# Latent keys normed and rotated right behind their projection, and the memory keys' transposes moved behind the third head pair's values, in a two-layer mixer and FFN kernel

## The chip, the cores and the metric

One core of a Trainium2 chip runs the whole program. The metric is the time of one execution on the device in microseconds (us). Three runs of the kernel before took 1013.88, 1010.58 and 1015.88 us, median 1013.88; one more execution was taken with the hardware profiler, and all rows below come from it.

## The reference

256 tokens of width 1024, float32, pass two layers. The first is an FFN, a mixer of window attention and mLSTM, and a second FFN. The second layer, where the change lies, mixes gated linear attention (GLA, 4 heads) with latent attention (MLA, 8 heads), then attends to a memory of 256 tokens, and ends with a convolved FFN. What the change touches is this:

```python
q = to_heads(rms_norm_2(c_q, mla_q_a_norm[l]) @ mla_w_uq[l], MLA_HEADS)
kv = to_heads(rms_norm_2(c_kv, mla_kv_a_norm[l]) @ mla_w_ukv[l], MLA_HEADS)
k_nope, v = kv[..., :MLA_NOPE], kv[..., MLA_NOPE:]
k_rot = jnp.broadcast_to(k_pe[:, None], (b, MLA_HEADS, s, MLA_ROPE))
k = jnp.concatenate([k_nope, k_rot], axis=-1)
q = rms_norm_2(q, mla_q_norm[l])
k = rms_norm_2(k, mla_k_norm[l])
q = jnp.concatenate([q[..., :MLA_NOPE], rope(q[..., MLA_NOPE:], positions)], axis=-1)
k = jnp.concatenate([k[..., :MLA_NOPE], rope(k[..., MLA_NOPE:], positions)], axis=-1)
o_mla = from_heads(causal_block_attention(q, k, v))
...
xk = rms_norm_2(xkv[:, :, 0], xa_k_norm[l])
```

## The kernel before, in words

Every large product is made of weights that stream from memory as float32, are split into a high half on ScalarE (line 368) and a low half on VectorE (line 369), and are multiplied three times on TensorE: lines 388 to 393 where features lie on the partitions, lines 397 to 399 (`mm3n`) where tokens do. Vectors of reciprocal roots are worked out by eleven small steps on GpSimd (`rsqrt`, lines 450 to 465).

The change lies in `mix2_heads` (lines 1056 to 1370). The latents are projected first (line 1066). Then come the latent keys without their rotated part, `pk` (line 1129), whose squares are summed per head into half 1 of `ssq` (line 1133), and the latent queries `q` in two halves of four heads (loop at line 1134), whose squares are summed into half 0 (line 1141). Both halves get a norm term (line 1142) and share one reciprocal root, `rqk` (line 1143). Behind it `kn`, the normed keys of all heads, is written: the plain part from `pk` (line 1150), the rotated part from `kp` (line 1152). The queries are rotated in one go (line 1154); their root `rq` enters later, with the scores.

The heads are worked on in four pairs by three helpers. `turned` transposes a pair's queries and keys (line 1190) and copies them to `qT` on VectorE (line 1193) and to `kT` on ScalarE (line 1195). `scores` multiplies them (lines 1205 and 1206), adds mask and scale and finds maxima on VectorE (lines 1210 and 1211), and takes exponentials on ScalarE (lines 1214 and 1215). `values` transposes the weights (line 1227), copies them to `pT` on ScalarE (line 1229), multiplies them with the values (line 1234) and splits the result. Between these steps stand the dense products `og`, `uv` and `gv`, the memory's keys `xk` (`xa_keys`, line 1398), the GLA products with the chunk states `st` (lines 1311 to 1322), and the GLA outputs `po` (lines 1342 to 1346). `xa_turn` (line 1415) transposes the memory's keys (line 1421) and copies them to `xkT` (line 1422), which the cross attention after this stage reads.

PSUM is dealt from two pools. `pa()` gives one bank out of four (tag "at"); the products of the latent keys and queries, the transposes and the scores use it. `bank()` gives one half of a two-bank tile out of two such tiles (tag "mm"), in the order in which the code calls it; the dense products, `xa_turn`, the states and `po` use it.

The order on each engine is not that of the text. The program is built in a context that simulates the time of every instruction (line 1582); whichever instruction is ready, has its buffer and comes first in the text is put next on its engine. `queued` (line 319) adds a rule to that: what is traced inside it on an engine comes behind the engine's instruction that was traced last before it. Each engine then works through its own queue in order. The weights' DMAs are issued by SP (line 354).

Of the kernel before, what the change touches and what calls it, by code (L numbers as in the profile page):

```python
# [14 lines left out]
AF = mybir.ActivationFunctionType  # L15
ALU = mybir.AluOpType
AX = mybir.AxisListType
PSUM = bass.MemoryType.PSUM

P = 128  # L20
# [3 lines left out]
TB = T // P  # L24
# [163 lines left out]
class Builder:  # L188
# [867 lines left out]
    def mix2_heads(self, mp, ot, xs, ms):  # L1056
        nc = self.nc
        V = nc.vector
# [4 lines left out]
        H = 8  # L1063


        ps = self.lin_n("lat", 432, xs)
# [9 lines left out]
        cs_ = []  # L1076
# [20 lines left out]
        ad = mt([P, 2, TB], "ad")  # L1097
# [28 lines left out]
        q = mt([P, TB, H, 96], "q")  # L1126
        ssq = mt([P, 2, TB, H], "ssq")
        rqk = mt([P, 2, TB, H], "rqk")
        pk = self.lin_n("uk", 512, cs_[:1], 1, pool=self.pa)
        for b in range(TB):  # L1130
            s2 = self.tmp([P, 512], "z")
            nc.scalar.activation(s2, pk[b], AF.Square)
            V.tensor_reduce(ssq[:, 1, b, :], s2.rearrange("p (h d) -> p h d", h=H), op=ALU.add, axis=AX.X)
        for c in range(2):
            ps = self.lin_n(f"uq{c}", 384, cs_[1:], 2, pool=self.pa)
            for b in range(TB):
                qb = q[:, b, 4 * c:4 * c + 4, :].rearrange("p h d -> p (h d)")
                nc.scalar.activation(qb, ps[b][:, :384], AF.Copy)
                s2 = self.tmp([P, 512], "z")
                nc.scalar.activation(s2[:, :384], ps[b][:, :384], AF.Square)  # L1140
                V.tensor_reduce(ssq[:, 0, b, 4 * c:4 * c + 4], s2[:, :384].rearrange("p (h d) -> p h d", h=4), op=ALU.add, axis=AX.X)
        V.tensor_tensor(ssq, ssq, ad[:, :, :, None].to_broadcast([P, 2, TB, H]), ALU.add)
        self.rsqrt(rqk, ssq, [P, 2, TB, H])
        rq, rk = rqk[:, 0], rqk[:, 1]
        kp = mt([P, TB, 32], "kp")
        self.rope(kp, cz[:, :, 384:416], "gk", lambda t: t, [P, TB, 32])
        rkp = mt([P, TB, H], "rkp")
        V.tensor_tensor(rkp, rk, fp[:, :, None].to_broadcast([P, TB, H]), ALU.mult)
        for b in range(TB):
# [1 line left out]
                            rk[:, b, :, None].to_broadcast([P, H, 64]), ALU.mult)  # L1151
            V.tensor_tensor(kn[:, b, :, 64:96], kp[:, b, None, :].to_broadcast([P, H, 32]),
                            rkp[:, b, :, None].to_broadcast([P, H, 32]), ALU.mult)
        self.rope(q[:, :, :, 64:96], q[:, :, :, 64:96], "gq", lambda t: t[:, :, None, :].to_broadcast([P, TB, H, 32]), [P, TB, H, 32])


        w2 = mt([16, T], "w2")
# [41 lines left out]
        def scores(qT, hp):  # L1199
            qT, kT = qT  # L1200
            out = []
            for i in range(2):
                h = 2 * hp + i
                ps = self.pa()
                nc.tensor.matmul(ps[:, 0:P], qT[:, i * T:i * T + P], kT[:, i * T:i * T + P], start=True, stop=True)
                nc.tensor.matmul(ps[:, P:3 * P], qT[:, i * T + P:i * T + T], kT[:, i * T:i * T + T], start=True, stop=True)
                S = mt([P, 3 * P], "S2", bufs=3)
                m = self.tmp([P, TB], "m2")
                wm = self.wmask.rearrange("p a k -> p (a k)")
                V.tensor_tensor_reduce(S[:, 0:P], ps[:, 0:P], wm[:, P:2 * P], rq[:, 0, h:h + 1], -3.0e38, ALU.add, ALU.max, m[:, 0:1])  # L1210
                V.tensor_tensor_reduce(S[:, P:3 * P], ps[:, P:3 * P], wm[:, 2 * P:4 * P], rq[:, 1, h:h + 1], -3.0e38, ALU.add, ALU.max, m[:, 1:2])
                V.tensor_scalar(m, m, -1.0, None, ALU.mult)
                l = self.tmp([P, TB], "l2")
                nc.scalar.activation(S[:, 0:P], S[:, 0:P], AF.Exp, bias=m[:, 0:1], accum_out=l[:, 0:1])
                nc.scalar.activation(S[:, P:3 * P], S[:, P:3 * P], AF.Exp, bias=m[:, 1:2], accum_out=l[:, 1:2])
                V.reciprocal(l, l)
                V.tensor_scalar(S[:, 0:P], S[:, 0:P], l[:, 0:1], None, ALU.mult)
                V.tensor_scalar(S[:, P:3 * P], S[:, P:3 * P], l[:, 1:2], None, ALU.mult)
                out.append(S)
            return out  # L1220

        def values(hp, Ss):
            pTs = []
            for i in range(2):
                pt = self.pa()
                for k in range(3):
                    nc.tensor.transpose(pt[:, k * P:k * P + P], Ss[i][:, k * P:k * P + P], self.ident)
                pT = mt([P, 3 * P], "pT2", bufs=2)
                nc.scalar.activation(pT, pt[:, :3 * P], AF.Copy)
                pTs.append(pT)  # L1230
            po = self.pa()
            for q0, kb, first, last in ((0, 0, True, True), (P, 0, True, False), (P, 1, False, True)):
                for i in range(2):
                    nc.tensor.matmul(po[64 * i:64 * i + 64, q0:q0 + P], vv[:, kb, 2 * hp + i, :],
                                     pTs[i][:, kb * P + q0:kb * P + q0 + P], start=first, stop=last)
            ms[4 + hp] = ot([P, 2, T], f"mla{hp}", dt=F32R)
            self.split(ms[4 + hp], po[:, :T])
# [5 lines left out]
        ps = self.lin_n("og", 512, xs)  # L1243
        for b in range(TB):
            nc.scalar.activation(og[:, b, :], ps[b], AF.Copy, scale=rN[:, b:b + 1])
        ps = self.lin_n("uv", 512, cs_[:1], 1)
# [15 lines left out]
        ps = self.lin_n("gv", 512, xs)  # L1262
# [5 lines left out]
        xkT = ot([P, 4, T], "xkT")  # L1268
        kk = self.xa_keys(ts, g2)
# [27 lines left out]
        S2 = scores(q2, 2)  # L1297
        q3 = turned(3)
        values(1, S1)
        self.xa_turn(kk, xkT)  # L1300


        st = [None]
        for c in range(3):
            b, c2 = c // 2, c % 2
# [19 lines left out]

        S3 = scores(q3, 3)
        values(2, S2)


        for b in range(TB):  # L1330
# [6 lines left out]
        for b in range(TB):  # L1337
            pt = po[b]
            for j in range(2):
# [4 lines left out]
                for r in range(2):  # L1344
                    h = 2 * j + r
# [11 lines left out]
        for hp in range(2):  # L1357
            pt = self.pa()
            for i in range(2):
                for b in range(TB):  # L1360
                    h = 2 * hp + i
# [225 lines left out]
```

## Time and profile before

| what | value |
|---|---|
| median of three runs | 1013.88 us |
| lowest and highest run | 1010.58 and 1015.88 us |
| profiled execution | 1010.23 us |
| its span, from first to last instruction | 1008.5 us |
| TensorE, VectorE, ScalarE, GpSimd busy in it | 98%, 73%, 59%, 6% |
| mean granted TensorE clock | 0.996 of full speed |
| share of TensorE in the chain of work that ended last | 94% |

How to read it: PE is TensorE's matmuls, PEld its weight loads, which overlap them, DVE is VectorE, ACT ScalarE, POOL GpSimd. Times in rows are us from the start of the span. [...] A row such as `714.89 0.77 PE L1205 MATMUL at<-kT,qT ... x2 [3.24 <-DVE qT L1193]` says that from 714.89 on two matmuls of line 1205, from kT and qT into an "at" bank, ran for 0.77 us together, and that TensorE had been idle for 3.24 us before, until VectorE's line 1193 was done. Matmuls are pipelined and overlap, so the busy times of single ones add up to more than the time they take together.

### The profile page before, as it was taken

How to read it: one execution, taken by the hardware profiler on the slowest of the kernel's cores; microseconds unless marked ns; L12 is line 12 of the kernel's file. 1: busy time of each engine (PE TensorE's matmuls, PEld its weight loads, DVE VectorE, ACT ScalarE, POOL GpSimd, SP SyncE). 2: the span in 40 equal slices, each digit the busy share in tenths (PEclk: the TensorE clock that was granted, in tenths of full speed). 3: DMA queues.
4: the chain of work that ended last, by engine and by line, in shares of the span. 5: the costliest groups of instructions: out<-in, count | busy, mean ns of one | idle time of the engine just before them, and what ended most of it. 6: DMA issues, size and time to landing. Idle time of an engine off the chain costs nothing.

```text
span 1008.5 us, 15805 instructions
## 1 busy us (share of the span) xinstructions
PE 984.3 (98%) x5870; PEld 856.2 (85%) x5870; DVE 737.8 (73%) x1288; ACT 596.4 (59%) x1038; POOL 59.4 (6%) x195
## 2 busy tenths in 40 slices
PE   7999999999999999999999999999899999999998
PEld 6888888988677788888888888998789888888887
DVE  7777766668986577776777865778858668888662
ACT  7655544568854556545655644659846457666541
POOL 2100000010000010001000200012001301000000
PEclk9999999999999999999999999999899999999999
DMA  8655555555345345545555655556306336555550
GB/s 298 251 188 190 182 187 183 196 168 179 125 154 182 105 141 194 189 169 169 200 184 191 211 180 174 170 195 206 103 1 219 116 105 217 191 191 177 182 172 21
DMA packets 51405, 172.80 MB, mean 171 GB/s; under 512 B 6256, under 2 KB 7552, under 8 KB 51328
## 3 DMA queue, kind: packets, MB, share of 16 engines
q1 hardware_dynamic: 49536, 169.89, 49.5%
q10 hardware_dynamic: 1728, 1.88, 0.8%
q8 instruction: 46, 0.75, 0.3%
q14 instruction: 31, 0.25, 0.1%
q0 software_dynamic: 64, 0.02, 0.0%
HBM read 170.72 MB, written 1.05 MB: 170 GB/s over the span
## 4 chain that ended last, share of the span: by engine, by line
PE 94%; DVE 3%; ACT 1%; issue 1%; POOL 0%; DMA 0%; DVEq 0%; ACTq 0%
PE mm L392 41%; PE mm L393 21%; PE mm L397 3%; PE mm L398 3%; PE mm L399 3%; PE mm L389 3%; PE mm L388 3%; PE mm L390 3%; PE at L392 2%; PE at L748 1%; PE at L708 1%; DVE wl L369 1%; PE at L393 1%; ACT wh L368 1%; PE at L740 1%
## 5 line engine op out<-in xcount | busy, mean ns | idle before, releaser
L369 DVE TENSOR_TENSOR wl<-wr,wh 128x1024 fp32r<-128x1024 f32 (+5 forms) x376 | 389.9, 1051 | 193.6 <-ACT wh L368 189.0
L368 ACT ACTIVATE wh<-wr 128x1024 fp32r<-128x1024 f32 (+5 forms) x376 | 339.1, 918 | 312.6 <-PE mm L392 149.0
L392 PE MATMUL mm<-xs,wh 128*128 128x512 f32 x1264 | 444.4, 395 | 2.4 <-DVE s L546 1.5
L393 PE MATMUL mm<-xs,wl 128*128 128x256 f32 x1264 | 354.8, 281 | 0.0
L392 PEld LDWEIGHTS mm<-xs,wh 128*128 128x128 f32 x1264 | 237.0, 187 | 58.2 <-issue 2.4
L393 PEld LDWEIGHTS mm<-xs,wl 128*128 128x128 f32 x1264 | 238.8, 189 | 0.5 <-issue 0.3
L392 PE MATMUL mm<-ahl,wh 128*128 128x512 f32 x396 | 138.3, 394 | 0.0
L393 PE MATMUL mm<-ahl,wl 128*128 128x256 f32 x396 | 111.0, 280 | 0.0
L392 PEld LDWEIGHTS mm<-ahl,wh 128*128 128x128 f32 x396 | 74.2, 187 | 17.0
L393 PEld LDWEIGHTS mm<-ahl,wl 128*128 128x128 f32 x396 | 74.9, 189 | 0.0
L397 PE MATMUL mm<-wh,xs 128*128 128x512 f32 (+2 forms) x160 | 61.0, 381 | 0.0
L398 PE MATMUL mm<-wl,xs 128*128 128x512 f32 (+2 forms) x160 | 61.0, 381 | 0.0
L399 PE MATMUL mm<-wh,xs 128*128 128x512 f32 (+2 forms) x160 | 60.7, 380 | 0.0
L392 PE MATMUL mm<-b,wh 128*128 128x512 f32 x128 | 45.4, 395 | 0.0
L390 PE MATMUL mm<-ahl,wl 128*128 128x256 f32 x132 | 37.4, 283 | 0.0
L389 PE MATMUL mm<-ahl,wh 128*128 128x256 f32 x132 | 37.4, 283 | 0.0
L388 PE MATMUL mm<-ahl,wh 128*128 128x256 f32 x132 | 37.3, 283 | 0.0
L393 PE MATMUL mm<-b,wl 128*128 128x256 f32 x128 | 36.5, 285 | 0.0
L398 PEld LDWEIGHTS mm<-wl,xs 128*128 128x128 f32 x160 | 30.1, 188 | 6.1 <-issue 1.1
L397 PEld LDWEIGHTS mm<-wh,xs 128*128 128x128 f32 x160 | 30.1, 188 | 6.1 <-issue 1.1
L399 PEld LDWEIGHTS mm<-wh,xs 128*128 128x128 f32 x160 | 30.1, 188 | 5.8 <-issue 0.8
L392 PE MATMUL at<-xs,wh 128*128 128x512 f32 x64 | 24.6, 423 | 8.9 <-ACT wh L368 6.6
(537 smaller groups left out, 1444.6 us busy)
## 6 DMA issues: line engine op xcount, KB each, us to landing
wr<-in_wts SPq DMA_DIRECT2D x288, 512.0 KB, 4.0
wr<-in_wts SPq DMA_DIRECT2D x26, 384.0 KB, 3.4
wr<-in_memt SPq DMA_DIRECT2D x4, 512.0 KB, 3.8
wr<-in_wts SPq DMA_DIRECT2D x4, 432.0 KB, 3.3
bb<-in_rows ACTq DMA_DIRECT2D x6, 256.0 KB, 4.1
wr<-in_wts SPq DMA_DIRECT2D x4, 272.0 KB, 2.5
x<-in_xt SPq DMA_DIRECT2D x4, 256.0 KB, 4.9
first<-in_wts SPq DMA_DIRECT2D x4, 256.0 KB, 4.9
```

Of the source, the lines that this page charges most:

```text
L368: nc.scalar.activation(hi[:, i:i + m], v[:, i:i + m], AF.Copy)
L369: nc.vector.tensor_tensor(lo[:, i:i + m], v[:, i:i + m], hi[:, i:i + m].bitcast(F32), ALU.subtract)
L388: mm(ps, wh, xs[:, 0, :], start=start, stop=False)
L389: mm(ps, wh, xs[:, 1, :], start=False, stop=False)
L390: mm(ps, wl, xs[:, 0, :], start=False, stop=stop)
L392: mm(ps, wh, xs, start=start, stop=False)
L393: mm(ps[:, T:], wl, xs[:, 0, :], start=False, stop=stop)
L397: mm(ps, xh, wh, start=start, stop=False)
L398: mm(ps, xh, wl, start=False, stop=False)
L399: mm(ps, xl, wh, start=False, stop=stop)
L708: nc.tensor.matmul(ps[h][:, i * nk:i * nk + nk], aq[p][g * per + i][hs, b * P:b * P + P], ak[p][hs, 0:nk], start=True, stop=True)
L740: nc.tensor.transpose(pt[:, j * P:j * P + P], Ss[h][:, j, kb * P:kb * P + P], self.ident)
```

## The change

It does two things. The norm term, the root, the rotation and the writing of `kn` move in front of the loop over the queries, with a root of their own; the queries' norm term and root stay behind the loop, for them alone, and the queries are rotated in two halves of four heads inside the loop. And `xa_turn` moves from behind the second pair's values to behind the third pair's, with its transposes tied to come after TensorE's last instruction traced before.

```diff
@@ -1131,6 +1131,19 @@
             s2 = self.tmp([P, 512], "z")
             nc.scalar.activation(s2, pk[b], AF.Square)
             V.tensor_reduce(ssq[:, 1, b, :], s2.rearrange("p (h d) -> p h d", h=H), op=ALU.add, axis=AX.X)
+
+        rq, rk = rqk[:, 0], rqk[:, 1]
+        V.tensor_tensor(ssq[:, 1], ssq[:, 1], ad[:, 1, :, None].to_broadcast([P, TB, H]), ALU.add)
+        self.rsqrt(rk, ssq[:, 1], [P, TB, H])
+        kp = mt([P, TB, 32], "kp")
+        self.rope(kp, cz[:, :, 384:416], "gk", lambda t: t, [P, TB, 32])
+        rkp = mt([P, TB, H], "rkp")
+        V.tensor_tensor(rkp, rk, fp[:, :, None].to_broadcast([P, TB, H]), ALU.mult)
+        for b in range(TB):
+            V.tensor_tensor(kn[:, b, :, 0:64], pk[b].rearrange("p (h d) -> p h d", h=H),
+                            rk[:, b, :, None].to_broadcast([P, H, 64]), ALU.mult)
+            V.tensor_tensor(kn[:, b, :, 64:96], kp[:, b, None, :].to_broadcast([P, H, 32]),
+                            rkp[:, b, :, None].to_broadcast([P, H, 32]), ALU.mult)
         for c in range(2):
             ps = self.lin_n(f"uq{c}", 384, cs_[1:], 2, pool=self.pa)
             for b in range(TB):
@@ -1139,19 +1152,10 @@
                 s2 = self.tmp([P, 512], "z")
                 nc.scalar.activation(s2[:, :384], ps[b][:, :384], AF.Square)
                 V.tensor_reduce(ssq[:, 0, b, 4 * c:4 * c + 4], s2[:, :384].rearrange("p (h d) -> p h d", h=4), op=ALU.add, axis=AX.X)
-        V.tensor_tensor(ssq, ssq, ad[:, :, :, None].to_broadcast([P, 2, TB, H]), ALU.add)
-        self.rsqrt(rqk, ssq, [P, 2, TB, H])
-        rq, rk = rqk[:, 0], rqk[:, 1]
-        kp = mt([P, TB, 32], "kp")
-        self.rope(kp, cz[:, :, 384:416], "gk", lambda t: t, [P, TB, 32])
-        rkp = mt([P, TB, H], "rkp")
-        V.tensor_tensor(rkp, rk, fp[:, :, None].to_broadcast([P, TB, H]), ALU.mult)
-        for b in range(TB):
-            V.tensor_tensor(kn[:, b, :, 0:64], pk[b].rearrange("p (h d) -> p h d", h=H),
-                            rk[:, b, :, None].to_broadcast([P, H, 64]), ALU.mult)
-            V.tensor_tensor(kn[:, b, :, 64:96], kp[:, b, None, :].to_broadcast([P, H, 32]),
-                            rkp[:, b, :, None].to_broadcast([P, H, 32]), ALU.mult)
-        self.rope(q[:, :, :, 64:96], q[:, :, :, 64:96], "gq", lambda t: t[:, :, None, :].to_broadcast([P, TB, H, 32]), [P, TB, H, 32])
+            q4 = q[:, :, 4 * c:4 * c + 4, 64:96]
+            self.rope(q4, q4, "gq", lambda t: t[:, :, None, :].to_broadcast([P, TB, 4, 32]), [P, TB, 4, 32])
+        V.tensor_tensor(ssq[:, 0], ssq[:, 0], ad[:, 0, :, None].to_broadcast([P, TB, H]), ALU.add)
+        self.rsqrt(rq, ssq[:, 0], [P, TB, H])
 
 
         w2 = mt([16, T], "w2")
@@ -1297,7 +1301,6 @@
         S2 = scores(q2, 2)
         q3 = turned(3)
         values(1, S1)
-        self.xa_turn(kk, xkT)
 
 
         st = [None]
@@ -1325,6 +1328,8 @@
 
         S3 = scores(q3, 3)
         values(2, S2)
+        with self.queued(nc.tensor):
+            self.xa_turn(kk, xkT)
 
 
         for b in range(TB):
```

## Rows read from the trace of the kernel before

**Rows 1.** The page of the kernel before, busy time by engine

```profile
PE 984.3 (98%) x5870; PEld 856.2 (85%) x5870; DVE 737.8 (73%) x1288; ACT 596.4 (59%) x1038; POOL 59.4 (6%) x195
```

**Rows 2.** 10 us stages: us; busy PE, PEld, DVE, ACT, POOL; PE clock; DMA share; GB/s

```profile
680.00:690.00 10.00, 10.00 (x48) 8.60 (x47) 7.31 (x14) 10.00 (x23) 1.52 (x3) 1.00 0.59 204
690.00:700.00 10.00, 10.00 (x47) 7.77 (x46) 9.85 (x20) 8.57 (x19) 5.58 (x13) 1.00 0.60 201
...
710.00:720.00 10.00, 6.76 (x33) 5.85 (x32) 8.38 (x32) 7.81 (x34) 2.32 (x11) 0.69 0.38 127
720.00:730.00 10.00, 9.58 (x99) 7.72 (x98) 9.23 (x36) 7.30 (x21) 0.00 (x0) 0.96 0.01 2
```

**Rows 3.** Timeline of TensorE: start, us, what, [idle before, releaser]

```profile
698.16 0.60 PE L1190 MATMUL at<-ident,q 128*96 128x128 f32 x4
...
706.33 0.60 PE L1190 MATMUL at<-ident,kn 128*96 128x128 f32 x4
...
711.05 0.60 PE L1190 MATMUL at<-ident,kn 128*96 128x128 f32 x4
714.89 0.77 PE L1205 MATMUL at<-kT,qT 96*128 96x128 f32 x2 [3.24 <-DVE qT L1193]
...
725.79 1.04 PE L1421 MATMUL mm<-ident,g2k 128*128 128x128 f32 x8
...
729.81 0.67 PE L1342 MATMUL mm<-st,qz 128*128 128x256 f32 x2 [0.42 <-issue]
...
743.43 0.38 PE L388 MATMUL mm<-mla,wh 128*128 128x256 f32 x1 [0.47 <-ACT mla L486]
```

**Rows 4.** 1 us stages around TensorE's stall, columns as in rows 2

```profile
714.00:715.00 1.00, 0.11 (x1) 0.14 (x1) 1.00 (x3) 0.50 (x2) 0.00 (x0) 0.50 0.00 0
...
720.00:721.00 1.00, 1.00 (x8) 1.00 (x6) 1.00 (x2) 0.74 (x3) 0.00 (x0) 0.64 0.06 16
721.00:722.00 1.00, 1.00 (x23) 0.83 (x22) 1.00 (x8) 1.00 (x3) 0.00 (x0) 1.00 0.00 0
```

**Rows 5.** Timeline of VectorE, the latents' stretch

```profile
674.95 1.33 DVE L1133 TENSOR_REDUCE ssq<-z 128x8 f32<-128x512 f32 x2
...
680.68 0.55 DVE L1141 TENSOR_REDUCE ssq<-z 128x4 f32<-128x384 f32 x1 [1.68 <-ACT z L1140]
...
684.15 1.29 DVE L369 TENSOR_TENSOR wl<-wr,wh 128x512 fp32r<-128x512 f32 x2 [0.90 <-ACT wh L368]
...
688.10 0.42 DVE L991 TENSOR_TENSOR rope<-q,ssgq 128x256 f32<-128x256 f32 x1
...
689.83 0.69 DVE L993 TENSOR_TENSOR q<-q,ccgq 128x512 f32<-128x512 f32 x1
...
696.66 1.28 DVE L1150 TENSOR_TENSOR kn<-at,rqk 128x512 f32<-128x512 f32 x2
...
700.45 0.76 DVE L1152 TENSOR_TENSOR kn<-kp,rkp 128x256 f32<-128x256 f32 x2
```

**Rows 6.** Timeline of VectorE, the heads' stretch

```profile
714.00 0.74 DVE L1193 TENSOR_SCALAR qT<-at,gqk 96x512 f32<-96x512 f32 x1
...
735.10 1.24 DVE L1322 SCALAR_TENSOR_TENSOR st<-st,g2k,mm 64x128 f32<-64x128 f32 x4 [1.08 <-PE mm L1311]
```

**Rows 7.** Timeline of GpSimd: first and last step of two reciprocal roots

```profile
690.70 0.60 POOL L454 TENSOR_SCALAR rqk<-ssq 128x32 int32<-128x32 int32 x1 [4.69 <-DVE ssq L1142]
...
696.18 0.35 POOL L465 TENSOR_TENSOR rqk<-rs02x2x,rqk 128x32 f32<-128x32 f32 x1
...
715.58 0.20 POOL L454 TENSOR_SCALAR xrk<-ks 128x8 int32<-128x8 int32 x1 [18.41 <-DVE m L1212]
...
718.53 0.20 POOL L465 TENSOR_TENSOR xrk<-rs02x,xrk 128x8 f32<-128x8 f32 x1
```

**Rows 8.** Timeline of ScalarE

```profile
726.43 1.27 ACT L1422 ACTIVATE xkT<-mm,xqk 128x512 f32<-128x512 f32 x2 [0.63 <-PE mm L1421]
...
741.10 0.94 ACT L1229 ACTIVATE pT<-at 128x384 f32<-128x384 f32 x2
```

More of the change, by code (lines that the diff above doesn't have):

```diff
@@ L1133, in mix2_heads @@
             V.tensor_reduce(ssq[:, 1, b, :], s2.rearrange("p (h d) -> p h d", h=H), op=ALU.add, axis=AX.X)
-        for c in range(2):
-            ps = self.lin_n(f"uq{c}", 384, cs_[1:], 2, pool=self.pa)
-            for b in range(TB):
[L1137 to L1141, printed above, removed]
-        V.tensor_tensor(ssq, ssq, ad[:, :, :, None].to_broadcast([P, 2, TB, H]), ALU.add)
-        self.rsqrt(rqk, ssq, [P, 2, TB, H])
         rq, rk = rqk[:, 0], rqk[:, 1]
+        V.tensor_tensor(ssq[:, 1], ssq[:, 1], ad[:, 1, :, None].to_broadcast([P, TB, H]), ALU.add)
+        self.rsqrt(rk, ssq[:, 1], [P, TB, H])
         kp = mt([P, TB, 32], "kp")
@@ L1153, in mix2_heads @@
                             rkp[:, b, :, None].to_broadcast([P, H, 32]), ALU.mult)
-        self.rope(q[:, :, :, 64:96], q[:, :, :, 64:96], "gq", lambda t: t[:, :, None, :].to_broadcast([P, TB, H, 32]), [P, TB, H, 32])
+        for c in range(2):
+            ps = self.lin_n(f"uq{c}", 384, cs_[1:], 2, pool=self.pa)
+            for b in range(TB):
+                qb = q[:, b, 4 * c:4 * c + 4, :].rearrange("p h d -> p (h d)")
+                nc.scalar.activation(qb, ps[b][:, :384], AF.Copy)
+                s2 = self.tmp([P, 512], "z")
+                nc.scalar.activation(s2[:, :384], ps[b][:, :384], AF.Square)
+                V.tensor_reduce(ssq[:, 0, b, 4 * c:4 * c + 4], s2[:, :384].rearrange("p (h d) -> p h d", h=4), op=ALU.add, axis=AX.X)
+            q4 = q[:, :, 4 * c:4 * c + 4, 64:96]
+            self.rope(q4, q4, "gq", lambda t: t[:, :, None, :].to_broadcast([P, TB, 4, 32]), [P, TB, 4, 32])
+        V.tensor_tensor(ssq[:, 0], ssq[:, 0], ad[:, 0, :, None].to_broadcast([P, TB, H]), ALU.add)
+        self.rsqrt(rq, ssq[:, 0], [P, TB, H])
         w2 = mt([16, T], "w2")
```

## The prediction

> **What bounds the kernel now.** I read the page's busy times first: TensorE is busy 98% of the span [rows 1], so only what stops or slows TensorE can move the end. Then the 10 us stages: from 680 to 700 TensorE has no idle time; from 710 to 720 it is busy 6.76 of 10 us at a mean clock of 0.69, and from 720 to 730 9.58 at 0.96 [rows 2]. The timeline of TensorE names the cause: the key transposes of the second head pair (line 1190) start at 711.05 and last 0.60, and the next score product (line 1205) starts at 714.89 after 3.24 us idle, released by the copy qT (line 1193) [rows 3]. That copy is on VectorE, which starts it only at 714.00 [rows 6], at the end of a queue that was full: 9.85 of 10 us busy between 690 and 700 [rows 2]. [...] After that I find two short gaps of 0.42 and 0.47 [rows 3]. **All there is to win here is 3.24 + 2.9 + 0.42 + 0.47 = 7.0 us.**
>
> Why is the head work late? The keys' squared sums are ready after two reductions that begin at 674.95 and last 1.33, so at 676.28, but the joint root waits for the last query sum: GpSimd starts it at 690.70 and ends at 696.53 [rows 7]. Only then can kn be written (696.66 and 700.45) [rows 5]. Until it is, the two key products pk hold two of the four one-bank "at" accumulators. The first query transposes start at 698.16 [rows 3], right behind the 1.28 us of line 1150 that free these banks at 697.94 [rows 5]; the key transposes follow only at 706.33 [rows 3].
>
> **Part 1, keys ahead of the queries.** Nothing of TensorE, ScalarE or SP is added or taken away; no DMA moves, and SP's queue is passed by nothing. On GpSimd one root of 32 values per partition becomes two of 16, each 11 steps. I have no row of 16: the root of 8 takes 718.73 - 715.58 = 3.15 us, the one of 32 5.83 [rows 7], and I take 4 to 4.5 between them. The keys' root then runs from about 676.5 to 681, where GpSimd has no other work but three zero fills (its 1.52 us in 680 to 690) [rows 2]; behind it stands the queries' root, which still begins near 689.5 and ends by 692.7 to 695.4 (3.15 to 5.83), not later than now. So nothing that waits for it, the scores first, loses.
>
> On VectorE kn (1.28 + 0.76 = 2.04 us) moves from 696.66 and 700.45 to about 681 to 684 [rows 5]. VectorE had gaps there of 1.68 and 0.90 [rows 5], with ScalarE solid (10.00 of 10) and 2.69 us of VectorE free in 680 to 690 [rows 2]; weight halves pushed back by the keys meet that slack, not TensorE. Half the query rotation moves ahead too. A step of 256 values takes 0.42 and one of 512 takes 0.69 [rows 5]: 0.27 per 256, so 0.285 for 128 and a fixed part of 0.15. The rotation was 2 x 0.42 + 2 x 0.69 = 2.2; half of it, 1.1, leaves the full stretch behind 690. In all 2.04 + 1.1 = **3.1 us come out of VectorE's queue ahead of the copy that TensorE waited 3.24 for**. Added are four rotation steps and one addition of the norm term, 5 x 0.15 = 0.75 us at most.
>
> At the rows' 0.15 each, 3.1 - 0.75 = 2.35 us net leave the queue, and 2.35 is the figure that I carry on. [...]
>
> The larger effect is order. With the two banks free near 684 instead of 697.94, and the first four heads' queries rotated by then, the transposes of pairs 0 and 1 and their copies can run some 12 us earlier, between the dense products, whose order the planner sets by readiness. Then qT of pair 1 exists before the dense products end, and the scores can start when the queries' root ends, near 695, not near 709. I take the whole 3.24 as gone, and with it the half clock: -3.24 - 2.9 = -6.1. If only the queue's own relief counted, 0.9 of the 3.24 would stay (a rival below). What is late next is VectorE's head work: it was 8.38 and 9.23 of 10 busy in 710 to 730 [rows 2], so TensorE may meet it again in gaps under 1 us.
>
> **Part 2, the memory keys' transposes.** The eight transposes take 1.04 us at 725.79 [rows 3], their two copies 1.27 on ScalarE [rows 8]. Their reader is the cross attention behind this stage, so nobody waits. They now follow the third pair's value products in TensorE's order. TensorE's sum is unchanged; 1.04 us leave the middle, where the heads' chains use it. At the end the copies become ready just when the last pair's pT copies (0.94 at 741.10) are due [rows 8]; ahead of these, they delay the chain to the last value product by up to 1.27. Against it stands the 0.47 gap at 743.43 [rows 3], which the transposes may fill. Bounds: -0.47 to +1.27; I take +0.6, towards the dear end, since the code's order puts the copies ahead.
>
> **Sum.** -6.15 + 0.6 = -5.5. The profiled execution took 1010.23 (1008.5 span and 1.7 around it): 1004.7 for one like it. The median of the runs, 1013.88, lies 3.65 higher, so the forecast is **1008.3**.
>
> **Rivals.**
> - *The stall only shrinks* (0.32). The planner may put other VectorE work, halves of weights wanted later above all, where the keys were. Then the queue is 2.35 lighter, 0.9 us of the stall stays and the clock still falls: -2.35 + 0.6 = -1.75, **1012.1**. For it speaks VectorE's fullness; against it that the transposes waited for banks, not for the queue alone. If the planned order doesn't change at all, which is the change not doing what it says, 1013.9.
> - *The gap splits but the clock falls all the same* (0.08). The score groups leave TensorE many short gaps instead of one; 2.9 us of half clock stay: -3.24 + 0.6 = -2.6, **1011.2**. Against it: the 0.42 gap lies in the stage from 720 to 730, whose 0.96 is what the first 0.72 us at half speed make by themselves [rows 2, 4], so that gap brought no second fall. [...]
> - *Accumulators in the wrong order* (0.14), the slow side. bank() deals two-bank tiles in the order of the code, and there are two of them. Before, the tile of the outputs po took over from one with a transposed pair of memory keys and the first state. Now it takes over from the tile of both later states, and the transposes' tile comes between. If it must wait for these states, it starts not at 729.81 [rows 3] but after the additions that end at 735.10 + 1.24 = 736.3 [rows 6]: 6.5 us, with the 2.9 of half clock behind a gap so long, 9.4. On the partial gain that is 1012.1 + 9.4 = **1021.5**; on the full one 1017.7. It decides if TensorE has nothing else in 730 to 736; against it: pairs 1 to 3 have scores and values due there, which fill most of it.
>
> **How the numbers follow.** What a measurement of this kernel can tell from no change is about 0.5%, 5.1 us: below 1008.8 is faster, above 1019.0 slower. The forecast has 0.46 and counts as faster; the shrunken stall and the falling clock, 0.40, as the same; the accumulators, 0.14, as slower. Range: below, all 7.0 us gone without a price, 1006.9, less the 3.3 by which the lowest run lies under the median: 1003.5. Above, nothing gained, the 0.6 paid, and the 2.0 by which the highest run lies over the median: 1016.5. That leaves out the slow rival and little else. The forecast's own range is 1004 to 1011.
>
> **What would show it.** Right: line 1150 ends before 686 and the first query transposes start before 692; the first line 1205 comes before 700; no TensorE gap over 1 us between 700 and 745; clock 1.00 in every stage there. Wrong: a gap at line 1205 still released by line 1193, a stage at 0.50, or a gap before lines 1342 or 388 near 730 to 743 released by line 1422 or 1322. An end of this stage that is 5 us earlier with a span that is not would mean that the cross attention or the last FFN gave it back.

## The result and the profile after

The changed kernel took 1022.75 us (median of four runs, 1021.36 to 1024.5), the kernel before beside it 1014.34. The ratio of their runs on record is 1.0100, with an interval of 1.0078 to 1.0123; the two medians by themselves give 1.0083. It is **slower**, outside the range of the forecast. The profiled execution took 1023.8 us with a span of 1022.0. Line numbers behind the change are higher by 3 to 5; 1193 (qT) is now 1197, 1205 is 1209, 1342 is 1347, 1421 is 1426.

Spans can't be compared to a microsecond: outside the stage of the change they ran from 856.1 to 862.8 us over the 18 profiles of this study. So I measure the **stage**: from the layer's first product of line 515 to its last product of line 390 on `os`, behind the cross attention. In the kernel before these rows are

```profile
663.01 0.95 PE L515 MATMUL at<-ones,g2k 128*128 128x1 f32 x8
...
814.73 0.28 PE L390 MATMUL at<-os,wl 128*128 128x256 f32 x1
```

so 151.72 us, and in the changed kernel 664.95 and 825.77, 160.82 us: 9.1 us more, between the 8.4 of the two medians and the 10.1 of the ratio. "+52" below means 52 us behind the first of these rows. The page of the changed kernel, then its 10 us stages (columns as in rows 2):

```profile
PE 994.1 (97%) x5870; PEld 860.2 (84%) x5870; DVE 738.9 (72%) x1293; ACT 595.1 (58%) x1038; POOL 66.6 (7%) x206
```

```profile
690.00:700.00 10.00, 10.00 (x50) 8.35 (x49) 10.00 (x22) 9.87 (x18) 5.45 (x6) 1.00 0.67 220
710.00:720.00 10.00, 8.64 (x52) 7.12 (x50) 8.67 (x31) 8.30 (x37) 0.00 (x0) 1.00 0.52 179
720.00:730.00 10.00, 7.09 (x72) 5.26 (x72) 9.04 (x28) 6.08 (x21) 3.66 (x11) 0.78 0.16 53
730.00:740.00 10.00, 10.00 (x52) 6.98 (x51) 6.79 (x28) 4.43 (x15) 0.00 (x0) 0.54 0.01 2
740.00:750.00 10.00, 10.00 (x76) 8.95 (x75) 0.85 (x2) 5.24 (x22) 0.00 (x0) 1.00 0.00 1
750.00:760.00 10.00, 6.33 (x31) 5.84 (x31) 6.05 (x17) 2.29 (x6) 2.19 (x11) 0.66 0.01 2
```

Where rows 2 had one stage with idle time and half clock, there are now two places: 715 to 740 and 750 to 760. TensorE's timeline shows what it waited for:

```profile
694.16 0.60 PE L1194 MATMUL at<-ident,q 128*96 128x128 f32 x4
694.59 0.60 PE L1194 MATMUL at<-ident,kn 128*96 128x128 f32 x4
...
702.09 0.39 PE L1209 MATMUL at<-kT,qT 96*128 96x128 f32 x2
...
718.24 0.43 PE L1238 MATMUL at<-pT,vv 128*64 128x128 f32 x2 [1.36 <-ACT pT L1233]
...
723.85 0.93 PE L1291 MATMUL mm<-qz,g2k 64*64 64x64 f32 x16 [0.51 <-DVE am L1298]
726.41 1.12 PE L1314 MATMUL mm<-gv,g2k 64*64 64x128 f32 x8 [1.62 <-DVE g2k L1417]
728.30 1.12 PE L1314 MATMUL mm<-gv,g2k 64*64 64x128 f32 x8 [0.78 <-DVE am L1298]
...
739.97 0.66 PE L1426 MATMUL mm<-ident,g2k 128*128 128x128 f32 x4
740.47 0.60 PE L1347 MATMUL mm<-st,qz 128*128 128x256 f32 x2
...
753.83 0.99 PE L1367 MATMUL at<-ident,czog 128*128 128x128 f32 x2 [3.63 <-DVE czog L1361]
```

Set beside [rows 3]: the keys' transposes of the first pair come 11.7 us earlier (694.59 for 706.33), and the stall of 3.24 at the second pair's scores is gone. In its place stand 1.36 + 0.51 + 1.62 + 0.78 = 4.27 us of gaps between 716 and 730. The outputs `po` start at 740.47, right behind the first half of the memory keys' transposes, where they started at 729.81. And a gap of 3.63 has come in at 753.83, where the GLA outputs are late. For every kernel below I added up, from 1 us stages between +46 and +100, TensorE's idle time and an estimate of what the half clock cost (busy time times one minus the granted clock): 4.20 + 2.91 before, 7.94 + 8.90 after, so **9.7 us more, 3.7 idle and 6.0 of clock**, against a stage longer by 9.1.

### The profile page after: what moved, and what is told of

It is laid out like the page before. It is cut to its first block, busy times and chain, and to the rows that moved or that the text cites. A ratio compares the mean times of both kernels' runs of the same rounds, so it can differ in the third digit from the quotient of the medians.

```text
span 1022.0 us, 15820 instructions
## 1 busy us (share of the span) xinstructions
PE 994.1 (97%) x5870; PEld 860.2 (84%) x5870; DVE 738.9 (72%) x1293; ACT 595.1 (58%) x1038; POOL 66.6 (7%) x206
## 4 chain that ended last, share of the span: by engine, by line
PE 94%; DVE 3%; ACT 1%; POOL 1%; issue 1%; DMA 0%; DVEq 0%; ACTq 0%
PE mm L392 41%; PE mm L393 21%; PE mm L397 3%; PE mm L398 3%; PE mm L399 3%; PE mm L388 3%; PE mm L389 3%; PE mm L390 3%; PE at L392 2%; PE at L748 1%; PE at L708 1%; PE at L393 1%; DVE wl L369 1%; PE at L1238 1%; PE at L740 1%
```

## The experiments

In short (stage, idle and clock cost from the profiled execution; the ratio from the timed runs):

| kernel | ratio to before, interval | stage | idle | clock |
|---|---|---|---|---|
| before | | 151.72 | 4.20 | 2.91 |
| after | 1.0100, 1.0078 to 1.0123 | 160.82 | 7.94 | 8.90 |
| e1_keys_only | 1.0062, 1.0035 to 1.0089 | 156.11 | 5.39 | 5.02 |
| e2_turn_only | 1.0062, 1.0039 to 1.0084 | 157.59 | 9.50 | 3.38 |
| e3_turn_at_banks | 1.0012, 0.9993 to 1.0031 | 153.55 | 4.90 | 4.61 |
| e4_turn_last | 1.0025, 1.0006 to 1.0045 | 155.01 | 6.18 | 4.61 |
| e5_states_at_banks | 1.0040, 1.0020 to 1.0061 | 157.34 | 7.89 | 4.33 |
| e6_gate_late | 1.0021, 1.0000 to 1.0041 | 153.42 | 4.61 | 4.72 |
| e7_states_and_gate | 1.0013, 0.9997 to 1.0030 | 155.53 | 6.03 | 4.70 |
| e8_turn_only_at_banks | 0.9981, 0.9966 to 0.9996 | 150.49 | 3.97 | 2.79 |
| e9_keys_no_scale | 1.0021, 0.9995 to 1.0047 | 150.30 | 3.40 | 1.70 |
| e10_late_no_scale | 0.9990, 0.9968 to 1.0011 | 149.02 | 4.02 | 1.70 |
| e11_keys_scale_on_act | 1.0061, 1.0034 to 1.0087 | 157.97 | 5.87 | 6.78 |
| e12_late_scale_on_act | 0.9989, 0.9967 to 1.0011 | 150.01 | 4.16 | 1.71 |
| e13_keys_rotation_whole | 1.0005, 0.9986 to 1.0024 | 150.81 | 3.06 | 3.41 |
| e14_late_rotation_split | 1.0055, 1.0032 to 1.0079 | 157.50 | 4.44 | 8.50 |
| e15_keys_early_turn_early_at_banks | 1.0054, 1.0032 to 1.0076 | 152.93 | 4.88 | 2.81 |
| e16_before_turn_at_banks | 1.0000, 0.9977 to 1.0023 | 149.92 | 4.89 | 0.00 |

### The two parts alone

e1_keys_only is the changed kernel with `xa_turn` back in its old place; e2_turn_only is the kernel before with `xa_turn` moved.

```diff
 e1:      values(1, S1)
+        self.xa_turn(kk, xkT)
...
         values(2, S2)
-        with self.queued(nc.tensor):
-            self.xa_turn(kk, xkT)
```

> The keys moved as in the change, the memory keys' transposes back in their old place. Theory A, tile order: the transposes' two-bank tile stands ahead of the tile of po and binds it to the third pair's values; that made the idle 3.63 us near 750 and the 5.6 us of half clock behind it, 6.5 us. Then po's first product is back near 732 to 734, no gap over 1 us near 750, and the time is 1022.75 - 6.5 = about 1016, with the gaps at 716 to 729 still there. Rival B, late heads: po is late because the earlier heads push everything behind them on ScalarE and VectorE; then this run stays at 1021 to 1024.

> The keys and queries as before the change, only the transposes moved behind the third pair's values. Theory A: po's first product falls behind the transposes, at about 741 instead of 729.81, a gap of 3 to 4 us opens before line 1362 of before, and the time is 1014.3 + 6.5 = about 1021. Rival B: the transposes have nobody waiting for them, so the time is 1014, within 2.

Each costs 0.62% alone, and their stages, +4.4 and +5.9, make 10.3 together, near the 9.1 of the whole. For e2_turn_only this is what theory A had. For e1_keys_only it is not: `po` is back at 731.16 and the gap near 750 is gone, as A said, but A's 1016 would have been 0.16% over the kernel before, because it put nothing down for the first part itself. e2_turn_only shows the second part's price by itself:

```profile
737.09 0.87 PE L1234 MATMUL at<-pT,vv 128*64 128x128 f32 x10 [0.64 <-ACT pT L1229]
737.88 0.66 PE L1422 MATMUL mm<-ident,g2k 128*128 128x128 f32 x4
738.38 0.60 PE L1343 MATMUL mm<-st,qz 128*128 128x256 f32 x2
...
752.65 0.33 PE L1363 MATMUL at<-ident,czog 128*128 128x128 f32 x1 [3.93 <-DVE czog L1357]
```

`po` (line 1343 here) comes directly behind the transposes' first half, and at 748.7 TensorE has run out of work: `po`'s squares, their root and `czog` follow in a chain that nothing shortens.

### The tile that the transposes take

`bank()` deals two-bank tiles in the order of the code. Moved behind the third values, `xa_turn` has a whole tile that is dealt between the tile of the two later states and the tile of `po`, and `queued` ties the transposes behind those values. The two buffers are used in turn, so `po` now takes over the one of the later states, as the prediction says, and it has its turn only after the transposes have theirs. e3_turn_at_banks gives them a one-bank accumulator instead; e4_turn_last leaves the tile and moves them behind the fourth values, after `po`'s in the code; e8, e15 and e16 make e3's edit in e2_turn_only, in e1_keys_only and in the kernel before.

```diff
 def xa_turn(self, kk, xkT):
     for hp in range(2):
-        pt = self.bank()
+        pt = self.pa()
```

> The whole change, but the transposes take two one-bank tiles of the other pool, so that no two-bank tile stands ahead of po; their place in TensorE's order is that of the change. Theory A: po's first product near 733, no gap near 750, 1016, as with the keys alone. Rival B, or a cost of the place itself and not of the tile: 1021 to 1024.

> The whole change, but the transposes are behind the last pair's values, in the text and on TensorE, so that po's tile is dealt before theirs. Theory A: 1016 or a little above, since the output products' first tile now waits for the transposes' copies. Rival B: 1021 to 1024.

> The kernel before with the second part of the change alone (transposes behind the third heads' values), their tile from the one-bank accumulators: e2_turn_only without its cost of tile order. It and e3_turn_at_banks differ in the first part of the change alone. If the first part is worth nothing because the stall only moved: both at the same time, 1011 to 1013, and this one with the old stall of 3.2 us at line 1205 and the clock at 0.5 for 5 to 6 us. If the first part costs by itself (theory that e1_keys_only's +0.6% is its own): this one is 4 to 6 us faster than e3_turn_at_banks, about 1007. If the first part gains where tiles allow: this one is 2 us or more slower than e3_turn_at_banks.

> The first part of the change alone (as e1_keys_only), with the transposes' tile from the one-bank accumulators. If the tile is the cost of e1_keys_only (1.0062): like e3_turn_at_banks, 1.001. If not: 1.006.

> The kernel before with that one tile from the one-bank accumulators and nothing moved. If e8_turn_only_at_banks owes its 0.19% to the tile: as it, 0.998. If to the move: as before, 1.000.

The one line takes e2's 1.0062 to e8's 0.9981 and the changed kernel's 1.0100 to e3's 1.0012. TensorE in e8_turn_only_at_banks:

```profile
714.56 0.77 PE L1205 MATMUL at<-kT,qT 96*128 96x128 f32 x2 [3.25 <-DVE qT L1193]
...
727.09 0.67 PE L1343 MATMUL mm<-st,qz 128*128 128x256 f32 x2
...
738.21 1.09 PE L1422 MATMUL at<-ident,g2k 128*128 128x128 f32 x8
```

`po` starts 11 us ahead of the transposes, which have kept their late place, and the gap at `czog` is gone. So the move itself costs nothing; **the tile order costs 0.8%, some 8 us**. e4_turn_last, which keeps the two-bank tile but has it dealt behind `po`'s, agrees: 1.0025. e16 shows that the tile without the move changes nothing that can be measured; e8's gain of 0.2% is too small to say more.

Two waits would fit the name "tile order": for the later states, whose buffer `po` takes over, or for the turn behind the transposes' tile. e3's and e8's edit alters both, since `po` then follows the first state instead. VectorE's timeline in the changed kernel shows that the states were not what held `po` on the chip:

```profile
734.83 1.24 DVE L1325 SCALAR_TENSOR_TENSOR st<-st,g2k,mm 64x128 f32<-64x128 f32 x4
```

These last additions ended at 736.07, and `po` started 4.4 us later, right behind the first transposes. In e2_turn_only the products that these additions take ended at 731.80; at the 1.24 us of the row above the additions were done near 733, by estimate, and TensorE still idled for 0.64 us later on (row 737.09 above), with `po` behind the transposes in its queue. That the planner put it there because of the turn is read from these rows; no run changes the turn alone.

In e15_keys_early_turn_early_at_banks the tile mends nothing that the times show (1.0054 beside e1's 1.0062), though its profiled stage is 3.2 us shorter; that is open. Beside e3's 1.0012 it says that with the keys early the late place of the transposes is itself worth 0.4%: the two parts are not independent, and why is open too. That e3 is 0.31% above e8, 3 us, is the first part's own cost where the transposes are late; the two intervals just touch, and 1.8 of the 3.1 us between the profiled stages are half clock.

### Is it the states' tile that stalls TensorE between +52 and +64?

In e3_turn_at_banks the gap of 1.63 waits for line 1417, which reads the memory keys' product out of the tile that the states need:

```profile
722.62 1.12 PE L1314 MATMUL mm<-gv,g2k 64*64 64x128 f32 x8 [1.63 <-DVE g2k L1417]
```

e5 gives the states one-bank accumulators (`pt = self.pa()` in their loop), e6 puts the output gates behind the heads' values (their loop inside `with self.queued(nc.vector, nc.scalar):`), and e7 does both.

> The changed kernel, with the transposes' tile (as in e3_turn_at_banks) and the three state products' tile too taken from the one-bank accumulators, so that the states wait neither for the memory keys' product tile nor for another state's copies. e3_turn_at_banks had gaps of 1.63 us (released by line 1417, which writes the memory keys) and 0.78 (line 1298) ahead of the states at 722 to 725, and the clock at 0.50 in 725 to 730. Theory C (tiles: the early stall only moved to the states because their tile is the one that the memory keys' product holds): both gaps go, no 5 us stage from 715 to 740 lies under 0.8, and the time is 5 to 7 us under e3_turn_at_banks, 0.5% or more under the kernel before (about 1006). Rival D (VectorE cannot keep up there, whatever tile is waited for): 2 us or more of gaps come back in 715 to 740, released by VectorE copies (lines 1197, 1298, 1325), the clock falls all the same, and the time is within 2 us of e3_turn_at_banks (about 1012).

> e3_turn_at_banks with the output gates' four steps (two tanh on ScalarE, two products on VectorE of about 0.65 us, line 1338) bound behind the heads' values instead of ahead of the memory keys. Theory C (tiles): the gap ahead of the states is released by the memory keys, so with 1.3 us less VectorE work ahead of them it shrinks from 1.63 by at most 1.3, but the clock may fall all the same; 1008 to 1012. Rival D (VectorE is the bound there): the sum of the gaps in 715 to 735 falls by about 1.3 from 3.9, and another gap of like size appears behind the heads' values, where the gates now are; time 1011 to 1014.

> Both edits together. Theory C: no more than e5_states_at_banks gives, since the states no longer wait for the memory keys (within 1.5 us of it). Rival D: 1.3 us or more better than e5_states_at_banks, since VectorE's queue is the bound and it is lighter by that.

Theory C falls. In e5 that gap went, and a larger one came, for a head's weights out of VectorE:

```profile
729.85 0.45 PE L1231 MATMUL at<-ident,S 128*128 128x128 f32 x1 [3.93 <-DVE S L1221]
```

D's time missed as well: e5 is 0.28% above e3, 2.8 us, where D had it within 2. Its edit takes banks from the pool that the heads use, so it does not test the states' tile alone. e7, with both edits, is 0.27% below e5, as D had it and C had not, and no better than e3. e6's gaps up to +64 shrank by 1.0, near the 1.3 that D had (0.28 + 0.85 + 0.51 + 1.50 for 4.10), and nothing was gained. The stretch from +58 to +63 suggests why, first in e3_turn_at_banks, then in e8_turn_only_at_banks:

```profile
719.16:724.16 5.00, 2.45 (x28) 1.70 (x26) 4.91 (x15) 2.13 (x9) 1.20 (x5) 0.84 0.34 107
```

```profile
720.67:725.67 5.00, 5.00 (x66) 3.96 (x68) 4.88 (x18) 3.04 (x9) 0.00 (x0) 1.00 0.02 5
```

VectorE is full in both. In e8 TensorE has work over from the stall; in e3 it has done that work between the dense products (which end at +50.4 instead of +46.1), and waits for VectorE at half load.

### Lighter work for VectorE

e9 and e10 leave out the division of the weights by their row sums, in e3 and in e8; e11 and e12 put the larger of its two scalings on ScalarE.

```diff
 e9, e10:
-    V.reciprocal(l, l)
-    V.tensor_scalar(S[:, 0:P], S[:, 0:P], l[:, 0:1], None, ALU.mult)
-    V.tensor_scalar(S[:, P:3 * P], S[:, P:3 * P], l[:, 1:2], None, ALU.mult)
 e11, e12:
-    V.tensor_scalar(S[:, P:3 * P], S[:, P:3 * P], l[:, 1:2], None, ALU.mult)
+    nc.scalar.activation(S[:, P:3 * P], S[:, P:3 * P], AF.Copy, scale=l[:, 1:2])
```

> e3_turn_at_banks without the division of the heads' scores by their row sums (one reciprocal and two scalings per head, lines 1220 to 1222): about 0.55 us of VectorE's queue for each of eight heads, 4.4 us, are left out of the heads' chains. Theory D (in the stretch from 50 to 68 us behind the first product of line 515 VectorE is the bound, and the keys' move only lets TensorE run out of work there earlier): the gap ahead of the states falls from 1.63 to under 0.7, the sum of gaps in that stretch from 4.1 to under 2.5, and the stage is 3 us or more shorter than e3's 153.55; beside e10_late_no_scale it is no longer slower, by within 1 us, or is faster. Rival E (the keys' move costs 3 us by something that VectorE's load does not set: the memory keys' products that come later on TensorE, or their root): the gap released by line 1417 stays over 1.3 us, and the stage stays 2.5 us or more longer than e10_late_no_scale's.

> e8_turn_only_at_banks (keys where they were) with the same division left out. Its gap of 3.25 us at line 1205 waits for a copy that stands behind the key gates' steps, ahead of any division, so both theories keep 3 us of it and the half clock behind it; the stage is 0 to 2 us shorter than e8's 150.49. With e9_keys_no_scale it tells the theories apart.

> e3_turn_at_banks with the larger of the two scalings of each head (line 1222, 256 values) on ScalarE: 8 x 0.26 us leave VectorE's queue, and 8 steps of about 0.4 us join ScalarE's, which is 2.1 to 5.0 of 5 us busy in the stretch. Theory D: the gaps from 50 to 68 us fall by 1 us or so, time 1 to 2 us under e3_turn_at_banks, if ScalarE keeps up; if it doesn't (it was full between 53 and 58), as e3 or 1 to 2 us slower. Rival E: as e3.

> The same for e8_turn_only_at_banks, which has no gap over 0.3 us between the stall and 110 us: under theory D no gain beyond 0.5 us, since TensorE is not waiting there; a candidate to beat both kernels all the same, by what the stall of 3.25 gives. 1010 to 1012.

e9's gaps did what D (VectorE's load sets them) said:

```profile
720.03 0.43 PE L1235 MATMUL at<-pT,vv 128*64 128x128 f32 x2 [2.12 <-ACT pT L1230]
...
728.73 0.65 PE L1311 MATMUL mm<-gv,g2k 64*64 64x128 f32 x8 [0.16 <-DVE g2k L1414]
```

0.16 ahead of the states for 1.63, 2.3 in all for 4.1, and a profiled stage shorter by 3.25. But the timed runs gained nothing: 1.0021 beside e3's 1.0012, and 0.31% above e10, just as e3 is 0.31% above e8. In three of e9's ten runs the mean clock was 0.987 to 0.990, in the others 0.996 to 0.998; the profiled one was of the others. The profiled stage is 1.28 above e10's, where D had it within 1. So with less work on VectorE 1.8 of the 4.1 us of gaps went; the 2.12 that stayed waits for a copy on ScalarE (line 1230), and that VectorE's load accounts for the time of the first part is not shown. ScalarE was no relief: with the larger scalings on it (e11) the gap ahead of the first values grew from 1.18 to 1.82, the clock fell twice (0.50 from +56 to +58 and from +66 to +75), and the ratio rose to 1.0061, 5 us above e3 and more than either theory had. e10 and e12 can't be told from the kernel before (0.9990 and 0.9989).

### The two halves of the first part

e13 is e3 with the query rotation in one piece again; e14 is e8 with the split rotation alone, root and keys as before the change. The split rotation stands inside the loop, so in the code it also comes ahead of the root and of `kn`.

```diff
 e14:
+            q4 = q[:, :, 4 * c:4 * c + 4, 64:96]
+            self.rope(q4, q4, "gq", lambda t: t[:, :, None, :].to_broadcast([P, TB, 4, 32]), [P, TB, 4, 32])
...
-        self.rope(q[:, :, :, 64:96], q[:, :, :, 64:96], "gq", lambda t: t[:, :, None, :].to_broadcast([P, TB, H, 32]), [P, TB, H, 32])
```

> e3_turn_at_banks with the query rotation in one piece behind both halves, as before the change; the keys' norm stays early. If the split costs (four more VectorE steps in the full stretch, and heads 0 to 3 ready early enough to push the memory keys' products back): 2 to 3 us less than e3_turn_at_banks, ratio to before about 0.998. If the keys' early norm is what costs: the first query transposes come later, the rest as in e3_turn_at_banks, gaps in the stretch from 52 to 64 us of 3 to 4 us in all, ratio about 1.001.

> e8_turn_only_at_banks (joint root, keys late) with the query rotation split alone. If the split costs: ratio 1.000 or more, with the old stall of 3.2 us. If the keys' early norm is what costs: as e8_turn_only_at_banks, 0.998, the stall kept, since the first transposes wait for accumulators that the keys hold.

The split alone takes e8 from 0.9981 to 1.0055. The old stall keeps about its length (3.55 for 3.25) and waits for another step of VectorE, and in this execution the clock then stayed low for 17 us; the rows are TensorE's, then two 10 us stages:

```profile
718.21 0.65 PE L1276 MATMUL mm<-ident,g2k 128*128 128x128 f32 x4 [3.55 <-DVE g2k L1258]
```

```profile
717.00:727.00 10.00, 8.70 (x53) 7.13 (x54) 8.42 (x31) 6.42 (x23) 2.74 (x11) 0.59 0.15 55
727.00:737.00 10.00, 10.00 (x55) 6.86 (x54) 4.49 (x17) 2.87 (x11) 0.00 (x0) 0.56 0.00 0
```

The keys' early norm without the split (e13) does remove that stall and ends where the kernel before is, 1.0005:

```profile
719.12 0.96 PE L1290 MATMUL mm<-qz,g2k 64*64 64x64 f32 x16 [1.27 <-ACT g2k L1280]
721.50 0.93 PE L1290 MATMUL mm<-qz,g2k 64*64 64x64 f32 x16 [0.94 <-DVE am L1297]
```

Two gaps of 2.2 us in all in place of 3.24, and a clock cost of 3.41 in place of 2.91. With the keys early, taking the split out shortens the profiled stage by 2.7 us, but the timed ratios (1.0005 and 1.0012) don't tell the two apart. So neither half of the first part gains, and the split loses where the keys are late. Why it loses so much there, when it adds four short steps, is not settled, nor is the part that its earlier place in the code has in it: 5.7 of the 7.0 us between the stages of e8 and e14 are half clock, and how much of that belongs to this one execution is open.

## Why the prediction was wrong, step by step

**"Nobody waits" for the moved transposes, bounds -0.47 to +1.27: wrong, and the largest miss.** I asked who reads `xkT`, and not whose tile is dealt behind the one that the transposes now hold. It is `po`'s. e2_turn_only puts the price at 0.62%, a stage longer by 5.9; e8_turn_only_at_banks takes it away without touching the move. The rival *accumulators in the wrong order* had the place, the kind of cost and nearly the time (1021.5). Its releaser was wrong: it let `po` wait for the later states, but these were done at 736.07, and the row at 740.47 stands behind the transposes at 739.97, which `queued` holds back until the third values. Against it I had put that pairs 1 to 3 would fill 730 to 736. They did fill it, at half clock, and the bill came at 753.83, when that work was used up. At 0.14 it was far too cheap for something that the text of the code fixes.

**"I take the whole 3.24 as gone, and with it the half clock": the first half came true, the sum did not.** kn was written early, as the timeline of VectorE in the changed kernel shows:

```profile
683.55 1.28 DVE L1143 TENSOR_TENSOR kn<-at,rqk 128x512 f32<-128x512 f32 x2
...
685.20 0.75 DVE L1145 TENSOR_TENSOR kn<-kp,rkp 128x256 f32<-128x256 f32 x2
```

Line 1143 ends before 686, as it should, and no gap waits for qT; the query transposes at 694.16 and the scores at 702.09 each missed their bound (692 and 700) by 2.1 to 2.2, of which 1.9 is the later start of the stage. But VectorE's work was only moved, and I had written myself that it was 8.38 and 9.23 of 10 busy behind the stall [rows 2]. I then priced what would be late next as "gaps under 1 us"; it was 4.27 us in four gaps. The rival *the stall only shrinks* was the nearest to this.

**The half clock as a fixed 2.9 that goes when the stall goes: wrong.** The kernel before shows the term in its 1 us stages: 0.50 from 714 on, full clock from 721 [rows 4], which makes 2.91. After the change it was 8.90 (6.0 between 725 and 740, 2.9 between 753 and 760), and in e1_keys_only 5.02. The rival *the gap splits but the clock falls all the same*, at 0.08, had this, and only kept the 2.9. Gaps of 0.51, 1.62 and 0.78 went with one fall, inside the 1.62, and a long low stretch, 0.50 in every 1 us stage from 726 to 739.

**The roots: bounds of 3.15 to 5.83 us, "the queries' root ends 692.7 to 695.4": wrong.** GpSimd's timeline in the changed kernel, the first step, the longest and the last:

```profile
694.14 0.57 POOL L454 TENSOR_SCALAR rqk<-ssq 128x16 int32<-128x16 int32 x1 [5.49 <-DVE ssq L1157]
...
697.15 2.56 POOL L459 TENSOR_TENSOR rqk<-rs02x,rqk 128x16 f32<-128x16 f32 x1
...
701.68 0.33 POOL L465 TENSOR_TENSOR rqk<-rs02x,rqk 128x16 f32<-128x16 f32 x1
```

7.87 us for 16 values, longer than the 5.83 for 32 [rows 7]. The first scores came at 702.09 instead of near 695. It cost TensorE nothing there, since it had dense products until +50.4.

**The split rotation at 0.75 us of VectorE at most: right as VectorE's load, wrong as a price.** In the changed kernel two steps of 128 values start 0.20 us apart (685.87 and 686.07), in the kernel before two of 256 start 0.33 apart (688.10 and 688.43): 0.13 per 128 and 0.07 fixed. At that, five steps add 0.35 us, under half of the 0.75. e14 makes the split 0.74% beside e8 all the same, with the clock in it, so the cost is not in the length of these steps; that it lies in what the changed readiness does to the order of the rest is not shown.

**What the sum would have been.** By the stages of the two parts alone, part 2 is +5.9 for +0.6 and part 1 is +4.4 for -6.1. On 1013.88 that gives 1024.2; measured 1022.75. That it comes so near is in part luck, since each stage is that of one execution and the parts are not independent.

## What to carry to other kernels

When a step that takes a buffer is moved in the code, list whose buffer was dealt behind its own before and whose is now, and what holds the step back: the price is the wait of the step that is dealt next, not of the reader (here 0.8% of the time). A stall that is released by an engine which is nine tenths busy behind it may only move when some of that engine's work is done earlier, as here from one gap of 3.24 us to four of 4.27 together: read what the engine still has to do until its load falls, and price the gaps there before counting the stall as won. And a steady half-clock price taken from one execution is a sample, not a term: behind one and the same stall it was 0.00 to 2.91 us here.

## What the runs showed of the hardware

**The clock after one and the same stall.** e16_before_turn_at_banks has the old stall at the same place and with the same length, but the clock never fell; its stall and its stages from there on:

```profile
715.01 0.46 PE L1205 MATMUL at<-kT,qT 96*128 96x128 f32 x2 [3.23 <-DVE qT L1193]
```

```profile
711.00:715.00 4.00, 0.78 (x8) 0.54 (x6) 4.00 (x14) 3.63 (x20) 0.00 (x0) 1.00 0.47 137
715.00:720.00 5.00, 4.04 (x26) 3.14 (x26) 4.09 (x18) 3.67 (x14) 2.47 (x11) 1.00 0.34 108
720.00:725.00 5.00, 4.81 (x60) 3.83 (x64) 4.88 (x18) 3.07 (x10) 0.00 (x0) 1.00 0.00 2
```

Six kernels have this stall of 3.23 to 3.25 us with nothing different ahead of it, and in their profiled executions paid 0.00 (e16), 1.70 (e10), 1.71 (e12), 1.71 (e2, in its first low stretch), 2.79 (e8) and 2.91 us (before) for it. Of 105 runs of the kernel before in the four groups of runs of this study, ten had a mean clock of 1.000, the others 0.995 to 0.998; the four runs of the changed kernel had 0.988 to 0.992.

**GpSimd beside a full VectorE.** The same step of line 459 on 16 values took 0.22 us in the keys' root, at 681.42 with VectorE idle, and 2.56 in the queries', at 697.15, while VectorE ran lines 369 and 490 back to back. It is no accident of one execution: in e3_turn_at_banks the step took 2.56 there too, at 693.38. The memory keys' root, 3.15 us before [rows 7], took 4.49 in the changed kernel. No VectorE instruction beside the 2.56 took over 0.7 us. And in the kernel before the same step on 32 values took 0.56 at 692.84, with line 369 at work on VectorE from 692.60 to 693.95. So what makes the 2.56 is not shown.
